# Token mixers of a hybrid decoder trunk: a head's last turns as a task of their own, beside the opening of the next head

## The chip, the cores and the metric

The kernel runs on 1 core of a Trainium2 chip, as one program in one launch. The metric is device time in microseconds (us), the median of the runs. A profiled execution of the kernel before is at hand: it names for each engine (PE is TensorE, DVE is VectorE, ACT is ScalarE, POOL is GpSimd, SP issues most transfers) each instruction with its start, its length and what it waited for.

## The reference, cut to what matters

One layer, a sequence of 1024 tokens, width 2048, all in float32:

```python
h = x @ w_in[i]                      # 15 column blocks of 512
y_a = short_conv_mixer(a_b, a_c, a_x, conv_w[i])
y_b = hgrn2_mixer(b_q, b_f, b_i, lower_bounds[i], hgrn_norm_g[i])      # 4 heads, state 128x128
y_c = diff_attn_mixer(c_q, c_k, c_v, lam, lam_init, diff_norm_g[i])    # 4 heads of 128
y_d = spatial_gate_mixer(gelu(d_u), gelu(d_v), ...)
y = concat([y_a * silu(g_a), y_b * silu(g_b), y_c * silu(g_c), y_d * silu(g_d)]) @ w_out[i]
x = layer_norm(ALPHA * x + y)
x = x + (p[i] @ w_pe[i]) * sigmoid(x @ w_pg[i])
```

`diff_attn_mixer` takes `softmax(q1 k1) - lam * softmax(q2 k2)`, causal, times v; `hgrn2_mixer` is a gated recurrence computed in blocks. The output of each head of B and of C goes through an RMS norm over its 128 channels before it is gated.

## The kernel before, in words

The three large products (`w_in`, `w_out`, `w_pg`) run as Strassen products: seven products of half matrices in place of eight, each of them as three matmuls of a high and a low part (`split`, lines 139 and 140: ACT casts a tile to `hi`, DVE subtracts to get `lo`). The `w_in` product runs in two stages. Stage one (up to some 690 us) takes four of the seven products for each of 30 groups of two column tiles (`PAIRS`) and puts the sums aside. Stage two (`second(g)`, 690 to 1430 us) takes the other three, of 24 matmuls each, and finishes the columns of group g. The order of `PAIRS` is C head 0, C head 1, the blocks of D, C heads 2 and 3, then for each j the B head j and the A channels j.

The token mixers are computed beside stage two. Each is a Python generator in `queue`; `products(..., every=2)` calls `step()` after every sixth matmul, and a step runs the generator at the head of the queue up to its next `yield`. So a stretch of mixer work stands behind every six matmuls of the product, 12 steps in a group, and a bare `yield` gives six matmuls of time to what went before. `unit_c(j)` and `unit_b(j)` enter the queue when their last columns are done (`kept(g, more)`). Only the head of the queue runs; a unit that enters waits until those ahead have ended.

A C head (`unit_c`, `mix_c`) loads its k, v and q tiles from DRAM (`back`, POOL's queue), waits 4 yields, splits k and q (casts L725, L726, L728, L737 on ACT, subtractions L727, L738 on DVE), transposes v (`turned`, L532), and then goes through eight blocks of queries: scores (L759, L760), softmax (L772, L782), transposes of the probabilities (`turn`, L791, into the tile `W`), times v (`values`, L798). At the end the gate is loaded (`gate_back`, L563), `rms(o, ss)` norms (L542 on DVE, a power on POOL L544, L545 on DVE), seven bare yields follow, and `finish` transposes the output (L552, tile `yt`), multiplies it with the gate (L554) and stores it to `y_dram` (L555). A B head (`unit_b`, `mix_b`) has the same frame around seven levels (L648 to L658, `gram` L617, L632), the transposes of its k (L532), and the state (`upd`, `hgo`, L681 to L703).

The tiles of one head are in the pool `work` under tags with one buffer each (`o`, `l1`, `q1`, `k1`, `v1`, `a1`, `x1`, `vt`, `W`) and `E` with two. A tile is written anew only when all who use what it held have ended, transfers included. In a C head `o` holds first the raw k and then the output; the gate is loaded to `l1` (C) or `v1` (B); a B head writes its product to `o` and keeps its output in an `E`.

The order on each engine is set when the program is built: the layer that builds it takes, for each engine, the instruction that stands first in the program among those that it holds to be ready by its own estimate; `early()` moves loads and splits of the large products ahead. Each engine then runs its list strictly in that order, whatever has really arrived.

After stage two the last unit (B head 3) runs on beside the first `w_out` product (L437, `tk`), and `drain()` puts out what is left of it before the tiles of A and B are loaded.

Of the kernel before, what the change touches and what calls it, by code (L numbers as in the profile page):

```python
# [38 lines left out]
def trunk_kernel(  # L39
# [79 lines left out]

    queue = []

    def step():
        while queue:
            if next(queue[0], queue) is not queue:
                return
            queue.pop(0)

    def drain():  # L130
        while queue:
            step()

    early = lambda: tc.high_priority(offset=4000)
# [330 lines left out]
    with tc.tile_pool(name="work", bufs=1) as work:  # L465
# [57 lines left out]
        def back(b, j, t):  # L523
            nc.gpsimd.dma_start(t, h_dram[b, j])
            return t
# [21 lines left out]
        def finish(o, norm, gt, y, kb):  # L547
            gt, y = ch(gt), ch(y)
            for b in range(2):
                ps = mx.tile([P, 4, P], F32, tag="mx", name="yt")  # L550
                for c in range(4):
                    T.transpose(ps[:, c, :], o[:, 4 * b + c, :], ident)  # L552
                c4 = slice(4 * b, 4 * b + 4)
                V.scalar_tensor_tensor(y[:, c4, :], ps, norm, gt[:, c4, :], op0=ALU.mult, op1=ALU.mult)  # L554
            nc.sync.dma_start(y_dram[kb].rearrange("p (c t) -> p c t", t=P), y)  # L555
# [5 lines left out]
        def gate_back(tag, k):  # L561
            gt = wt(tag)
            nc.gpsimd.dma_start(gt, g_dram[k])  # L563
            return gt
# [23 lines left out]
        def unit_b(j):  # L588
            k, f, qt, lw = wt("k1"), back(B_F, j, wt("l1")), back(B_Q, j, wt("q1")), wtE()
            iv = back(B_I, j, wtE())  # L590
            for _ in range(4):
                yield
            S.activation(k, f, AF.Sigmoid, scale=-1.0)
            S.activation(f, f, AF.Sigmoid)
            S.activation(k, k, AF.Copy, scale=one_lb[:, j : j + 1])
            V.tensor_scalar(f, f, one_lb[:, j : j + 1], lb[:, j : j + 1], op0=ALU.mult, op1=ALU.add)
            V.tensor_scalar_max(lw, f, SPLIT)
            V.tensor_scalar(f, f, F_FLOOR, SPLIT, op0=ALU.max, op1=ALU.min)
            S.activation(lw, lw, AF.Ln)
            S.activation(f, f, AF.Ln, scale=1.0 / SPLIT)  # L600
            V.tensor_tensor(f, f, lw, op=ALU.add)
            yield
            vtok = turned(wt("vt"), iv)
            yield
            yield from mix_b(j, k, f, qt, vtok)

        def mix_b(j, kt, lt, qt, vtok):
            at = ch(wt("a1"))
            G.memset(at, 0.0)

            def gram(li, m, ls, rs):
                if m >= 32:
# [58 lines left out]
            yield  # L671
            ktok = ch(wtV())
            transpose_to(ktok, ch(kt))
            o = ch(wtE())
            yield
            state = None
            ss = small.tile([P, 8], F32, tag="ss", name="ss")
            for b in range(2):
# [25 lines left out]
                S.copy(o[:, 4 * b : 4 * b + 4, :], pso)  # L704
                for c in range(4):
                    square(ss, 4 * b + c, pso[:, c, :])
            gt = gate_back("v1", 4 + j)
            rms(o, ss)
            for _ in range(7):
                yield  # L710
            finish(o, hg_g(j), gt, wt("o"), 4 + j)

        def unit_c(j):
            kraw, vraw, qraw = back(C_K, j, wt("o")), back(C_V, j, wtE()), back(C_Q, j, wtE())
            for _ in range(4):
                yield
            kh = [wt(t, dt=F32R) for t in ("l1", "q1")]
            kl = [wt(t, dt=F32R) for t in ("k1", "v1")]  # L720
            for mp in range(2):
                own = slice(64 * mp, 64 * mp + 64)
                oth = slice(64 - 64 * mp, 128 - 64 * mp)
                src, hi = kraw[own, :], kh[mp][own, :]
                S.copy(hi, src)  # L725
                S.copy(kh[mp][oth, :], src)  # L726
                V.tensor_tensor(kl[mp][own, :], src, hi.bitcast(F32), op=ALU.subtract)  # L727
                S.copy(kl[mp][oth, :], kl[mp][own, :].bitcast(F32))  # L728
            yield
            vtok = turned(wt("vt"), vraw)  # L730
            yield
            qs = [wt(t, dt=F32R) for t in ("a1", "x1")]
            for mp in range(2):
                own = slice(64 * mp, 64 * mp + 64)
                oth = slice(64 - 64 * mp, 128 - 64 * mp)
                src, hi = qraw[own, :], qs[mp][own, :]
                S.copy(hi, src)  # L737
                V.tensor_tensor(qs[mp][oth, :], src, hi.bitcast(F32), op=ALU.subtract)  # L738
            yield
            yield  # L740
            yield
            yield from mix_c(j, kh, kl, qs, vtok)

        def mix_c(j, kh, kl, qs, vtok):
# [59 lines left out]
            for i in range(NCH):  # L804
                a_t, rc = scores(i)
                yield
                if last is not None:
                    values(*last)
                if i >= 2:
                    yield  # L810
                last = (i, turn(i, a_t), rc)
                if i >= 4:
                    yield
            yield
            values(*last)
            gt = gate_back("l1", j)
            rms(o, ss)
            for _ in range(7):
                yield
            finish(o, da_g[:, j : j + 1], gt, gt, 8 + j)  # L820

        vd = []

# [400 lines left out]
```

## Time and profile before

| | us |
|---|---|
| median of 3 runs (2148.4 to 2153.97) | 2150.9 |
| the profiled execution's own time | 2151.72 |
| its span, first to last instruction | 2149.9 |
| PE busy of it | 2049.5 (95%) |
| DVE, ACT busy | 1393.3, 872.6 |
| stage two with the mixers, 690 to 1485 us: PE busy | 738.7 of 795 |

A busy PE is one with a matmul in it. Where PE is idle, the trace names what it waited for: an instruction of another engine or a transfer. An engine that runs its list in order and waits at its head also holds back all that stands behind it.

### The profile page before, as it was taken

To read this page: it belongs to the slowest core of one execution; us is meant where nothing else is said; L and a number is where in the kernel's file an instruction comes from. 1 tells how busy PE (TensorE), PEld (TensorE's weight loads), DVE (VectorE), ACT (ScalarE), POOL (GpSimd) and SP (SyncE) were. 2 spreads that over 40 slices of the span, in tenths; PEclk is the share of its full clock that TensorE was granted. 3 is DMA by queue.
4 is the path that set the end of the run, shared out by engine and by line. 5 is a ranking of instruction groups with operands and counts; after the bars stand their busy time and mean duration, and the time that the engine had idled before them with its cause. 6 is when DMAs were issued, how large, how long until landed. Compare 5 with 4: busy or idle time off the path is not lost. (4 is left out here: it accounts for less than half of the span.)

```text
span 2149.9 us, 25562 instructions
## 1 busy us (share of the span) xinstructions
PE 2049.5 (95%) x9708; PEld 1686.0 (78%) x9708; DVE 1393.3 (65%) x1763; ACT 872.6 (41%) x1287; POOL 150.2 (7%) x224
## 2 busy tenths in 40 slices
PE   7999999999999999988999989988999999999989
PEld 5788888878787777777878878867878788888867
DVE  7644545455465365756666778886767999455785
ACT  4322222222224256753555555553322245533432
POOL 0000101101010000010000000000121100000000
PEclk9999999999999999999999999999999999999999
DMA  6666767767778656467455364585677643433564
GB/s 236 238 201 219 265 229 266 268 236 258 250 261 306 224 168 194 128 216 250 156 166 195 124 208 145 195 307 195 238 280 254 233 167 102 153 98 99 189 204 136
DMA packets 169755, 443.81 MB, mean 206 GB/s; under 512 B 14432, under 2 KB 14576, under 8 KB 168352
## 3 DMA queue, kind: packets, MB, share of 16 engines
q1 hardware_dynamic: 120928, 293.05, 41.5%
q0 software_dynamic: 28064, 101.93, 13.3%
q10 hardware_dynamic: 20640, 47.19, 5.7%
q8 instruction: 76, 1.25, 0.3%
q14 instruction: 47, 0.39, 0.1%
HBM read 311.05 MB, written 131.07 MB: 206 GB/s over the span
## 5 line engine op out<-in xcount | busy, mean ns | idle before, releaser
L139 ACT CAST wh<-b 128x1024 fp32r<-128x1024 f32 x180 | 189.1, 1051 | 528.4 <-PE a L188 344.5
L437 PE MATMUL tk<-th,ah 128*128 128x512 f32 x832 | 327.0, 396 | 5.8 <-DVE z L967 3.0
L437 PE MATMUL tk<-th,al 128*128 128x512 f32 x832 | 325.8, 392 | 6.1 <-DVE al L140 5.9
L437 PE MATMUL tk<-tl,ah 128*128 128x512 f32 x832 | 322.7, 393 | 3.8 <-DVE tl L140 3.8
L140 DVE TENSOR_TENSOR wl<-b,wh 128x1024 fp32r<-128x1024 f32 x180 | 219.8, 1222 | 158.2 <-ACT wh L139 152.4
L437 PEld LDWEIGHTS tk<-th,ah 128*128 128x128 f32 x832 | 156.9, 189 | 40.5 <-issue 3.4
L437 PEld LDWEIGHTS tk<-th,al 128*128 128x128 f32 x832 | 157.0, 189 | 40.2 <-DVE al L140 9.0
L437 PEld LDWEIGHTS tk<-tl,ah 128*128 128x128 f32 x832 | 156.9, 189 | 38.0 <-DVE tl L140 5.0
L139 ACT CAST th<-t 128x1024 fp32r<-128x1024 f32 x64 | 67.4, 1054 | 206.5 <-PE tk L437 185.4
L262 DVE TENSOR_TENSOR b<-b,b 128x1024 f32<-128x1024 f32 x30 | 36.8, 1225 | 160.9 <-DMA b<-in_w_in_dram 160.9
L140 DVE TENSOR_TENSOR tl<-t,th 128x1024 fp32r<-128x1024 f32 x64 | 78.0, 1222 | 57.9 <-ACT th L139 57.8
L139 ACT CAST th<-b 128x1024 fp32r<-128x1024 f32 x48 | 50.6, 1053 | 140.6 <-PE tk L437 106.6
L188 PE MATMUL b<-N1h,wh 128*128 128x512 f32 x240 | 97.0, 404 | 7.5 <-ACT wh L139 7.5
L188 PE MATMUL a<-A22h,wl 128*128 128x512 f32 x240 | 96.2, 401 | 8.3 <-DVE wl L140 8.2
L188 PE MATMUL a<-S2h,wh 128*128 128x512 f32 x240 | 95.2, 397 | 6.3 <-ACT wh L139 5.3
L188 PE MATMUL a<-S2h,wl 128*128 128x512 f32 x240 | 95.1, 396 | 3.5 <-DVE wl L140 3.5
L188 PE MATMUL a<-S2l,wh 128*128 128x512 f32 x240 | 95.0, 396 | 3.4 <-DVE S2l L140 3.4
L188 PE MATMUL c<-A12h,wh 128*128 128x512 f32 x240 | 96.5, 402 | 1.7 <-ACT wh L139 1.7
L188 PE MATMUL b<-N1h,wl 128*128 128x512 f32 x240 | 96.5, 402 | 1.0 <-DVE wl L140 1.0
L188 PE MATMUL c<-A12h,wl 128*128 128x512 f32 x240 | 96.7, 403 | 0.0
L188 PE MATMUL c<-A12l,wh 128*128 128x512 f32 x240 | 96.4, 402 | 0.0
L188 PE MATMUL b<-N1l,wh 128*128 128x512 f32 x240 | 96.3, 401 | 0.0
(337 smaller groups left out, 4611.9 us busy)
## 6 DMA issues: line engine op xcount, KB each, us to landing
b<-in_w_in_dram SPq DMA_DIRECT2D x182, 512.0 KB, 4.6
stash<-ev ACTq DMA_DIRECT2D x60, 512.0 KB, 4.2
e<-stash SPq DMA_DIRECT2D x60, 512.0 KB, 4.7
s<-in_w_out_dram POOLq DMA_DIRECT2D x32, 512.0 KB, 7.4
ot<-s POOLq DMA_DIRECT2D x32, 512.0 KB, 5.5
h<-e SPq DMA_DIRECT2D x32, 512.0 KB, 4.6
t<-ot SPq DMA_DIRECT2D x32, 512.0 KB, 4.5
t<-b ACTq DMA_DIRECT2D x30, 512.0 KB, 3.9
```

Of the source, the lines that this page charges most:

```text
L139: S.copy(hi, raw)
L140: V.tensor_tensor(lo, raw, hi.bitcast(F32), op=ALU.subtract)
L188: T.matmul(ps, lhsT=w_[:, c], rhs=x_[k // 4][:, k % 4, :], start=(start and k == 0 and i3 == 0), stop=(k == 7 and i3 == 2), skip_group_che ...
L262: V.tensor_tensor(b22, b22, b12, op=ALU.add)
L437: T.matmul(ps[nn][m], lhsT=l[:, kk % 2, t], rhs=w[:, wi, :], start=(not cont and kk == 0 and i3 == 0), stop=(kk == 7 and i3 == 2), skip_gr ...
```

## The change

`finish` leaves the generators. When a head has normed its output, it puts `finish` with a counter of 9 into a new list `later`; `step()` counts it down and runs it 9 steps on, beside what the queue then does. One turn before its end a head calls `open_next()`, which runs the next generator in the queue, if there is one, up to its first `yield`: that is its loads. The opening yields become 5.

So that two heads can be open at once, the tiles move: a C head loads its raw k into `a1` (not `o`), the gate of B and C goes to `W`, where `finish` also writes the product; a B head keeps its output in `o` (not an `E`); `turns` starts from 0 in each B head, so that its first level takes `x1` and then `W`. In `unit_c` q is loaded ahead of v, and the transposes of v come after the split of q and three bare yields, with four behind them. No instruction of computation is added or taken away.

```diff
--- before.py
+++ after.py
@@ -119,16 +119,27 @@
 
 
 
-    queue = []
+    queue, later = [], []
 
     def step():
+
+        for todo in list(later):
+            todo[0] -= 1
+            if todo[0] == 0:
+                later.remove(todo)
+                todo[1]()
         while queue:
             if next(queue[0], queue) is not queue:
                 return
             queue.pop(0)
 
+    def open_next():
+
+        if len(queue) > 1:
+            next(queue[1])
+
     def drain():
-        while queue:
+        while queue or later:
             step()
 
     early = lambda: tc.high_priority(offset=4000)
@@ -588,7 +599,7 @@
         def unit_b(j):
             k, f, qt, lw = wt("k1"), back(B_F, j, wt("l1")), back(B_Q, j, wt("q1")), wtE()
             iv = back(B_I, j, wtE())
-            for _ in range(4):
+            for _ in range(5):
                 yield
             S.activation(k, f, AF.Sigmoid, scale=-1.0)
             S.activation(f, f, AF.Sigmoid)
@@ -607,6 +618,7 @@
         def mix_b(j, kt, lt, qt, vtok):
             at = ch(wt("a1"))
             G.memset(at, 0.0)
+            turns[0] = 0
 
             def gram(li, m, ls, rs):
                 if m >= 32:
@@ -671,7 +683,7 @@
             yield
             ktok = ch(wtV())
             transpose_to(ktok, ch(kt))
-            o = ch(wtE())
+            o = ch(wt("o"))
             yield
             state = None
             ss = small.tile([P, 8], F32, tag="ss", name="ss")
@@ -704,17 +716,16 @@
                 S.copy(o[:, 4 * b : 4 * b + 4, :], pso)
                 for c in range(4):
                     square(ss, 4 * b + c, pso[:, c, :])
-            gt = gate_back("v1", 4 + j)
+            open_next()
+            gt = gate_back("W", 4 + j)
             rms(o, ss)
-            for _ in range(7):
-                yield
-            finish(o, hg_g(j), gt, wt("o"), 4 + j)
+            later.append([9, lambda: finish(o, hg_g(j), gt, gt, 4 + j)])
 
 
 
         def unit_c(j):
-            kraw, vraw, qraw = back(C_K, j, wt("o")), back(C_V, j, wtE()), back(C_Q, j, wtE())
-            for _ in range(4):
+            kraw, qraw, vraw = back(C_K, j, wt("a1")), back(C_Q, j, wtE()), back(C_V, j, wtE())
+            for _ in range(5):
                 yield
             kh = [wt(t, dt=F32R) for t in ("l1", "q1")]
             kl = [wt(t, dt=F32R) for t in ("k1", "v1")]
@@ -727,8 +738,6 @@
                 V.tensor_tensor(kl[mp][own, :], src, hi.bitcast(F32), op=ALU.subtract)
                 S.copy(kl[mp][oth, :], kl[mp][own, :].bitcast(F32))
             yield
-            vtok = turned(wt("vt"), vraw)
-            yield
             qs = [wt(t, dt=F32R) for t in ("a1", "x1")]
             for mp in range(2):
                 own = slice(64 * mp, 64 * mp + 64)
@@ -736,9 +745,11 @@
                 src, hi = qraw[own, :], qs[mp][own, :]
                 S.copy(hi, src)
                 V.tensor_tensor(qs[mp][oth, :], src, hi.bitcast(F32), op=ALU.subtract)
-            yield
-            yield
-            yield
+            for _ in range(3):
+                yield
+            vtok = turned(wt("vt"), vraw)
+            for _ in range(4):
+                yield
             yield from mix_c(j, kh, kl, qs, vtok)
 
         def mix_c(j, kh, kl, qs, vtok):
@@ -811,13 +822,12 @@
                 last = (i, turn(i, a_t), rc)
                 if i >= 4:
                     yield
+            open_next()
             yield
             values(*last)
-            gt = gate_back("l1", j)
+            gt = gate_back("W", j)
             rms(o, ss)
-            for _ in range(7):
-                yield
-            finish(o, da_g[:, j : j + 1], gt, gt, 8 + j)
+            later.append([9, lambda: finish(o, da_g[:, j : j + 1], gt, gt, 8 + j)])
 
         vd = []
```

What stands on POOL where C head 0 ends and C head 1 opens, before (with buffer numbers; `h8_1`, `h6_1`, `h7_1` are v, q and k of head 1, `g_dram0` the gate of head 0):

```order
L563 DMA l1_5758<-g_dram0_97 128x1024
L524 DMA E_5828<-h8_1_4821 128x1024
L524 DMA E_5830<-h6_1_4825 128x1024
L544 ISA
L544 TENSOR_TENSOR rstd_5761<-ss_5211,nhalf_115 128x8
L524 DMA o_5826<-h7_1_4817 128x1024
```

The same place on POOL with the change:

```order
L535 DMA a1_5764<-h7_1_4817 128x1024
L535 DMA E_5766<-h6_1_4825 128x1024
L535 DMA E_5768<-h8_1_4821 128x1024
L574 DMA W_5795<-g_dram0_97 128x1024
L555 ISA
L555 TENSOR_TENSOR rstd_5798<-ss_5245,nhalf_115 128x8
```

The load of k stood behind the norm's power and waited for `o`; now it stands first, q ahead of v, and the gate goes to `W`.

PE at the same place, before: the last products ahead of the transposes of head 0's output and of head 1's v (`pv` of the last block is 40 product matmuls ahead):

```order
L188 MATMUL c_6068<-A12h_4676,wh 128x512
L188 MATMUL c_6068<-A12l_4678,wh 128x512
L188 MATMUL c_6068<-A12h_4676,wl 128x512
L552 MATMUL yt<-ident,o 128x128 x8
L532 MATMUL tr<-ident,E 128x128 x8
L188 MATMUL c_6068<-A12h_4676,wh 128x512
```

PE with the change, from that `pv` on:

```order
L809 MATMUL pv<-vt,W 128x128 x8
L199 MATMUL b_5673<-N4l_4759,wh 128x512
L199 MATMUL b_5673<-N4h_4757,wl 128x512
L199 MATMUL b_5673<-N4h_4757,wh 128x512
L199 MATMUL b_5673<-N4l_4759,wh 128x512
L199 MATMUL b_5673<-N4h_4757,wl 128x512
L199 MATMUL c_6068<-A12h_4675,wh 128x512
L199 MATMUL c_6068<-A12l_4677,wh 128x512
L199 MATMUL c_6068<-A12h_4675,wl 128x512
L543 MATMUL tr<-ident,E 128x128 x8
```

The transposes of v (`tr`) now come 8 product matmuls after the last `pv`; head 0's `yt` follows 33 more behind them, and head 1's first scores right behind it.

DVE where B head 0 makes its first level, before (`W` is the second tile of that level):

```order
L601 TENSOR_TENSOR l_8680<-l_8680,E 128x1024
L511 TENSOR_TENSOR e_20_8901<-b_8904,e_20_8901 128x512
L571 TENSOR_TENSOR e_20_8900<-e_20_8900,e_20_8901 128x1024
L140 TENSOR_TENSOR wl<-t_22_9294,wh 128x1024
L648 TENSOR_TENSOR x_8762<-q_8682,E 128x512
L649 TENSOR_TENSOR x_8762<-q_8682,E 128x512
L650 TENSOR_TENSOR W<-k_8679,E 128x1024
L658 TENSOR_TENSOR l_8680<-l_8680 128x512
```

DVE there with the change, from the norm of C head 3 on:

```order
L553 TENSOR_SCALAR ss<-ss 128x8
L556 TENSOR_TENSOR o<-o,rstd 128x1024
L565 SCALAR_TENSOR_TENSOR W<-yt,da_g,W 128x512
L612 TENSOR_TENSOR l_8558<-l_8558,E 128x1024
L565 SCALAR_TENSOR_TENSOR W<-yt,da_g,W 128x512
L151 TENSOR_TENSOR wl<-t_20_8972,wh 128x1024
L660 TENSOR_TENSOR x_8671<-q_8560,E 128x512
L661 TENSOR_TENSOR x_8671<-q_8560,E 128x512
L670 TENSOR_TENSOR l_8558<-l_8558 128x512
L522 TENSOR_TENSOR e_18_8591<-b_8594,e_18_8591 128x512
L662 TENSOR_TENSOR W<-k_8557,E 128x1024
L664 TENSOR_TENSOR E<-l_8558 128x256x2
```

The first level came long after C head 3's product with the gate; now it comes directly behind it and writes `W`, which that product has just filled for the store to `y_dram`.

PE at the end of B head 3, beside the `w_out` product, before:

```order
L437 MATMUL tk_10832<-tl,ah 128x512
L532 MATMUL tr<-ident,k_10531 128x128 x8
L681 MATMUL upd<-vt,W 128x128 x4
L686 MATMUL hgo<-vt,a_10609 128x128 x4
L703 MATMUL hgo<-state,q_10534 128x128 x3
L681 MATMUL upd<-vt,W 128x128 x3
L686 MATMUL hgo<-vt,a_10609 128x128 x4
L703 MATMUL hgo<-state,q_10534 128x128 x4
L552 MATMUL yt<-ident,E 128x128 x8
L437 MATMUL tk_11157<-th,ah 128x512
```

PE there with the change, right behind the last `hgo`:

```order
L448 MATMUL tk_10826<-th,al 128x512
L448 MATMUL tk_10826<-tl,ah 128x512
L448 MATMUL tk_10827<-th,ah 128x512
L448 MATMUL tk_10827<-th,al 128x512
L448 MATMUL tk_10827<-tl,ah 128x512
L448 MATMUL tk_10828<-th,ah 128x512
L448 MATMUL tk_10828<-th,al 128x512
L448 MATMUL tk_10828<-tl,ah 128x512
L448 MATMUL tk_10829<-th,ah 128x512
L448 MATMUL tk_10829<-th,al 128x512
L448 MATMUL tk_10829<-tl,ah 128x512
L563 MATMUL yt<-ident,o 128x128 x8
```

Eleven product matmuls of the `w_out` product now stand between the last state product and the transposes of the normed output.

## Rows read from the trace of the kernel before

**Rows 1.** Windows: PE, PEld, DVE, ACT, POOL busy us (instructions), granted clock, DMA share.

```profile
300.00:350.00 50.00, 50.00 (x222) 41.32 (x221) 27.57 (x24) 15.19 (x20) 6.28 (x10) 1.00 0.74 262
690.00:1485.00 795.00, 738.69 (x3901) 613.07 (x3901) 533.06 (x881) 429.13 (x751) 47.02 (x61) 0.97 0.57 191
1410.00:1455.00 45.00, 36.84 (x226) 30.51 (x227) 43.15 (x58) 22.03 (x28) 0.00 (x0) 1.00 0.85 300
1470.00:1485.00 15.00, 10.43 (x39) 8.76 (x40) 4.37 (x6) 2.58 (x9) 4.58 (x5) 0.77 0.56 176
```

**Rows 2.** Waits of PE, 690 to 1500 us: total, times, longest.

```profile
PE yt L552 <- DVE o L545: 7.8, 4, 3.2
PE yt L552 <- DVE E L545: 7.7, 3, 5.5
PE b L188 <- ACT wh L139: 7.5, 2, 4.7
PE gram L632 <- DVE x L650: 5.5, 2, 3.7
PE sc L759 <- DVE a L738: 4.7, 1, 4.7
PE sc L759 <- ACT l L726: 4.5, 2, 2.6
PE tk L437 <- DVE al L140: 3.6, 2, 2.9
PE gram L617 <- DVE W L657: 3.5, 1, 3.5
...
PE yt L552 <- ACT wh L139: 1.0, 1, 1.0
```

**Rows 3.** Timeline of PE, end of C head 0: start, length, engine, line.

```profile
832.12 1.06 PE L791 MATMUL att<-ident,E 128*128 128x128 f32 x8
833.47 2.05 PE L798 MATMUL pv<-vt,W 128*128 128x128 f32 x16
847.80 1.22 PE L552 MATMUL yt<-ident,o 128*128 128x128 f32 x8 [3.20 <-DVE o L545]
```

**Rows 4.** Timeline of POOL: loads of the next C head.

```profile
832.49 0.53 POOL L524 DMA_DIRECT2D E<-h  x1 [13.18 <-DMA e<-stash]
...
849.32 0.59 POOL L524 DMA_DIRECT2D o<-h  x1 [10.41 <-PE yt L552]
...
1081.50 0.53 POOL L524 DMA_DIRECT2D E<-h  x1 [7.95 <-DMA b<-in_w_in_dram]
```

**Rows 5.** Timeline of ACT: casts that waited for those loads.

```profile
841.20 1.05 ACT L737 CAST a<-E 64x1024 fp32r<-64x1024 f32 x1 [4.92 <-DMA E<-h]
...
1005.98 1.05 ACT L725 CAST l<-o 64x1024 fp32r<-64x1024 f32 x1 [7.20 <-DMA o<-h]
...
1087.73 1.04 ACT L737 CAST a<-E 64x1024 fp32r<-64x1024 f32 x1 [1.36 <-DMA E<-h]
```

**Rows 6.** Timeline of PE, end of B head 3.

```profile
1468.06 1.06 PE L703 MATMUL hgo<-state,q 128*128 128x128 f32 x8
1474.57 1.94 PE L552 MATMUL yt<-ident,E 128*128 128x128 f32 x8 [5.46 <-DVE E L545]
```

**Rows 7.** DMA issues of a kind: KB each, median us to landing.

```profile
E<-h POOLq DMA_DIRECT2D x16, 512.0 KB, 5.3
```

**Rows 8.** Line L555, the stores of a head's product.

```profile
DMA to landing us min/median/max: 2.7/5.7/7.1
```

**Rows 9.** Timeline of DVE, first level of B head 0.

```profile
1208.28 1.22 DVE L140 TENSOR_TENSOR wl<-t,wh 128x1024 fp32r<-128x1024 f32 x1
1209.87 0.69 DVE L648 TENSOR_TENSOR x<-q,E 128x512 f32<-128x512 f32 x1 [0.37 <-ACT E L646]
```

**Rows 10.** Timeline of SP's queue: a weight load and the transfer behind it.

```profile
743.07 0.39 SPq L173 DMA_DIRECT2D b<-in_w_in_dram  x1
755.86 0.32 SPq L490 DMA_DIRECT2D t<-t  x1
```

## The prediction, made before the change was run

> **What bounds the kernel now.** I read the windows first. In a stretch of products alone PE is busy for all of 50 us, with 222 matmuls, so 0.225 us for one. In the mixer stretch it is busy 738.7 of 795 us [rows 1]: TensorE is the bound, and 56 us of its idle time lie there. DVE (533 us) and ACT (429 us) have room in the mean, though not at the end, where DVE is busy 43.2 of 45 us. PE's work does not change, so the change can only move those 56 us, and the time in which the granted clock is down: it is 0.77 in the last window of rows 1, so part of it at 1.2 GHz, after a wait.
>
> Next, what the 56 us wait for [rows 2]. The transposes of a head's normed output (`yt`) have 7.8 + 7.7 + 1.0 = 16.5 us. The first scores of a C head (`sc`) have 4.7 + 4.5 = 9.2, and the split that ACT does late beside them (`b <- wh`) 7.5, of which I put some 1.7 to the opening of C head 2. The levels of the B heads and the product beside the last one have 5.5 + 3.5 + 3.6 = 12.6. The first two are what the change speaks of.
>
> Last, how one of them comes about. At the end of C head 0 PE has its last `pv` done at 833.47 + 2.05 = 835.5 and reaches `yt` at 844.6, and waits 3.20 us [rows 3]. ACT had stood 4.92 us for the next head's q, whose load POOL issued at 832.5 and which the cast took at 841.2, 8.7 us later [rows 4, 5]; DVE's subtraction for q stands ahead of the norm and waits with it. The load of k is issued only at 849.3, when `yt` has freed `o` [rows 4], so the first scores wait too. An engine that waits for a load holds back everything behind it, and these loads are slow.
>
> **The change part by part.** A step is six matmuls, 1.35 us. Counted in the code, a C head holds the queue for 35 steps before (4+1+1+3, 18 in the blocks, 1, 7) and 31 now until the next one is opened; a B head 39 and 32. But a unit can't start before its columns are done: B head 3 is opened at step 341 in both, and its levels begin at step 348 instead of 347. The queue's total is no shorter. What counts is where the order puts each instruction. All sums are against the profiled execution's own 2151.72 us (the span of 2149.9 and 1.8 around it), which is 0.8 above the median of 2150.9.
>
> *Waits of `yt`: -10.5.* For the four C heads `yt` now comes 41, 10, 10 and 10 product matmuls after the last `pv` and behind the eight transposes of the next tile (1.0 us), against 40, 18, 14 and 11; it is not later in matmuls, but the wait below comes ahead of it and covers the norm. I set the four at nothing (7.8 before). For the B heads the distance from the last state product is 16, 16, 54 and 11 matmuls and for the first of them 1.0 us of transposes as well, against 21, 19, 23 and 0. At the end of B head 3 the norm takes from 1469.1 to 1474.6 = 5.5 us with nothing to cover it [rows 6]; 11 x 0.225 = 2.5 now cover it, 3.0 stay. I leave 1.0, 2.0, 0 and 3.0. So 16.5 go to 6.0. Bounds: -14 (only the last stays) and -5 (half of them stay).
>
> *Transposes of the next v: +7.5.* These are new waits. The tile `E` is free when the last probabilities are transposed, or one instruction before, when DVE has read it; then the load is issued, and PE needs it after 0.45 + 2.05 + 1.8 = 4.3 us (C head 0: two products, `pv`, eight products), 4.3 (C head 2), 4.7 and 4.1 (before B head 0 and D, where the tile is free 1.1 earlier): 17.4 us of cover in all. Four loads at the median of 5.3 [rows 7] and 0.1 each to issue make 21.6, so 4.2 of waits; at the 8.7 of 832.5 to 841.2 they make 34.8, so 17.4. I take the 6.2 us from 1081.50 to 1087.73 [rows 4, 5], the opening of C head 3 and the less crowded of the two cases: 24.8 - 17.4 = 7.4, taken as 7.5. The Trainium skill (DMA: Bandwidth & Descriptors, Anatomy of one DMA) gives a transfer issued by GpSimd about 2.0 us and its bytes at 436 GB/s, an estimate of 3.2 us for 512 KB; by it these waits and 7.5 us of the sum would be gone. The trace disagrees: the median is 5.3 us. Its main page (Trainium Kernel Development and Optimization, Key Constraints) says that all queues share the same 16 DMA engines, so that an earlier issue brings no bandwidth; that fits the 8.7 us, and it would take the sum to the upper end.
>
> *First scores of a C head: -6.8.* k no longer waits for `o`. The opening of C head 0 stays, since its columns set it. That of C heads 1 and 3 stands 41 and 10 matmuls and two sets of transposes behind the last `pv`, with k loaded before: 4.5 go. C head 2 loses the 7.20 us in which ACT stood for k [rows 5], but its q is stored only some six steps before it is split, and a cast for it may stand ahead of a split again. Of 4.7 + 1.7 + 4.5 = 10.9 I leave 4.1. Bounds: 0 and -10.9.
>
> *Casts of the next k: +2.* On ACT they now stand ahead of the copies of the last probabilities (C heads 1 and 3). k's load can be issued when `a1` is free, after the last scores; at 6.2 us the cast holds ACT for some 1 us each time. Bounds: 0, and +5 at 8.7 us for both.
>
> *The tile `W`: +2.4.* The gate, the product and its store hold `W`, and the next head's first write of `W` waits for the store: two copies on ACT (C heads 1 and 3), two multiplications on DVE (B heads 0 and 1). Behind B head 0's stand the next split and the copies of the levels. The store takes 0.3 to issue and 5.7 [rows 8]; the order has one split of 1.2 and four instructions of 0.7 between [rows 9], 4 us: 2 us. The copies have 25 to 28 matmuls and the scores, 7 to 8 us, against 1.4 for the products and 6.0: 0.2 each. B head 1 has 70 matmuls. Bounds: 0 (the store at 2.7) and +8 (at 7.1, and held in SP's queue).
>
> *Levels of the B heads: -3.2.* Between the last `pv` of C head 3 and the last `yt` lie 838 matmuls before and 878 now, and the levels of B head 0 start 141 earlier, those of B head 3 14 earlier (3.2 us). Where DVE is full, that takes 3.2 us off the 12.6. Bounds: -8 and +2.
>
> The sum is -10.5 + 7.5 - 6.8 + 2 + 2.4 - 3.2 = -8.6: 2143.1, and 0.8 less for the median: 2142.3. I forecast 2142 us.
>
> **The rivals.** *The loads take the place of the norm: no change.* If the loads take 8.7 us, as at the first boundary, the new waits are 17.4 instead of 7.5: -8.6 + 9.9 = +1.3, 2152. For it: these openings load three tiles and a gate in a row. Against it: 6.2 at the other one. The same outcome, at 2148, if `open_next()` finds an empty queue where it matters: it does so at B heads 1 to 2 and 2 to 3.
>
> *The tile `W`: slower.* SP's queue can stand long ahead of a store: after the weight load at 743.07 the next transfer is issued at 755.86, 12.8 us later [rows 10]. A store of a product behind such a load holds `W`, then DVE or ACT, then the splits behind them. With 6.0 for the store less some 5 of work between, the engine stands 13.8; a product of 24 matmuls already split covers 5.4, so PE loses 8.4 at a place. At two of the four places that is +16.8, less the 2.4 I have counted: 2142 + 14 = 2156. It decides from some 5 us at two places. Against it: the stores before follow the product closely, and the loads in front of them are few.
>
> *More goes than I count:* loads at the median, no first scores that wait, nothing for k and `W`: -10.5 + 4.2 - 10.9 - 3.2 = -20.4, 2130.5.
>
> **How the numbers follow.** My case, -6.5 to -20, has 0.50. More than that 0.05. No change 0.25 (loads 0.18, empty queue 0.07). Slower 0.20 (`W` 0.14; 0.06 for the casts of k or q that hold ACT before more splits than I see). About 0.3%, 6.5 us, is what a measurement of this kernel can tell from no change. So faster 0.55, same 0.25, slower 0.20. The range that holds 8 in 10 reaches from 2129 to 2156; the likeliest case's own is 2131 to 2144.
>
> **What would show it.** In the profile after: PE's wait at `yt` for C heads under 1 us, 3 us at the last; a new wait of the transposes of v (`tr <- E`) of 1 to 4 us at the end of C heads 0 to 3; first scores of C heads 1 and 3 without a wait, and no cast of k that stands 7 us; the first level of B head 0 some 30 us earlier against the products, DVE standing about 2 us for a store there; PE idle from 690 to 1485 near 48 us instead of 56. I am wrong if DVE or ACT stand more than 5 us for `y_dram` at more than one place, if the waits of `tr` come to over 15 us, or if the last 60 us of stage two have as much idle time as before.

## The result and the profile after

The changed kernel takes 2126.48 us (median; 2126.28 to 2130.34), the kernel before 2149.65 beside it: ratio 0.9891, 95% interval 0.9862 to 0.9921. So it is faster, by 23 us where 8.6 were forecast, and below the range of 2129 to 2156.

Windows of the changed kernel: first two that answer to [rows 1], then the mixer stretch, from the first wait of stage two to the `yt` of B head 3.

```profile
690.00:1485.00 795.00, 753.79 (x3989) 626.28 (x3989) 547.33 (x898) 437.99 (x760) 46.23 (x61) 0.98 0.59 199
1410.00:1455.00 45.00, 40.43 (x253) 33.53 (x252) 35.52 (x48) 24.80 (x42) 3.70 (x4) 0.96 0.64 223
698.01:1449.04 751.03, 716.26 (x3840) 596.25 (x3841) 520.75 (x872) 425.03 (x746) 43.27 (x57) 0.98 0.57 194
```

The same stretch of the kernel before, cut at the same two instructions:

```profile
697.79:1474.57 776.78, 723.28 (x3840) 600.54 (x3841) 524.59 (x873) 421.77 (x742) 45.51 (x59) 0.97 0.56 188
```

Both do 3840 matmuls. The stretch is 25.7 us shorter: PE's idle time falls from 53.5 to 34.8 (-18.7), and its busy time by 7.0, at a granted clock of 0.98 for 0.97. The rest of the program is 3.9 us longer (2128.3 - 1449.04 against 2149.9 - 1474.57). DVE, full at the end of stage two before, is busy 35.5 of the 45 us there.

PE's waits of the changed kernel, 690 to 1500 us; they answer to [rows 2] (total, times, longest):

```profile
PE b L199 <- ACT wh L150: 11.4, 4, 3.5
PE yt L563 <- DVE o L556: 8.3, 4, 2.9
PE tr L844 <- DMA E<-h: 3.9, 2, 3.2
PE tr L543 <- DMA E<-h: 3.2, 2, 1.9
...
PE tk L448 <- ACT ah L150: 2.6, 1, 2.6
PE tk L448 <- DVE al L151: 2.2, 2, 1.2
...
PE gram L644 <- DVE W L669: 1.6, 1, 1.6
PE pv L809 <- ACT W L803: 1.3, 2, 0.8
PE gram L644 <- DVE W L662: 0.8, 1, 0.8
...
PE gram L629 <- DVE W L669: 0.3, 1, 0.3
```

No row of first scores is left, the levels (`gram`) have 2.7 us, and the new row is `tr` behind a load of `E`, 7.1 us in all. The product beside the last head (`tk`) waits no less than before, 4.8 us for 4.5; but 3.6 of them now come at 1475.98 and 1477.77, behind the last `yt`, and so lie in the 3.9 us above.

The timeline of PE and POOL where C head 0 ends; it answers to [rows 3, 4]:

```profile
824.55 0.53 POOL L535 DMA_DIRECT2D a<-h  x1 [81.39 <-DVE mxs L775]
...
835.01 0.53 POOL L535 DMA_DIRECT2D E<-h  x1 [9.92 <-DMA e<-stash]
835.99 0.53 POOL L535 DMA_DIRECT2D E<-h  x1 [0.45 <-PE att L802]
...
836.00 2.04 PE L809 MATMUL pv<-vt,W 128*128 128x128 f32 x16
...
841.18 1.09 PE L543 MATMUL tr<-ident,E 128*128 128x128 f32 x8 [1.30 <-DMA E<-h]
...
849.62 0.60 PE L563 MATMUL yt<-ident,o 128*128 128x128 f32 x4
```

k is asked for at 824.55 instead of 849.32, and `yt` no longer waits; v, asked for at 835.99, is waited for instead. The end of B head 3, which answers to [rows 6], waits 2.91 us instead of 5.46:

```profile
1449.04 1.94 PE L563 MATMUL yt<-ident,o 128*128 128x128 f32 x8 [2.91 <-DVE o L556]
```

One wait is new in a place that the prediction does not speak of, in B head 3. Timeline of POOL, DVE, ACT and PE:

```profile
1367.74 0.53 POOL L535 DMA_DIRECT2D q<-h  x1 [7.59 <-DMA h<-e]
...
1375.01 0.69 DVE L660 TENSOR_TENSOR x<-q,E 128x512 f32<-128x512 f32 x1 [7.25 <-DMA q<-h]
...
1377.53 0.70 ACT L666 ACTIVATE E<-l 128x512 f32<-128x512 f32 x1 [11.19 <-DVE W L662]
1378.11 1.06 ACT L150 CAST wh<-t 128x1024 fp32r<-128x1024 f32 x1
...
1379.22 0.50 PE L199 MATMUL b<-N1h,wh 128*128 128x512 f32 x1 [3.52 <-ACT wh L150]
```

The columns of q have only just been stored (`h<-e`) when POOL loads them: the mixers have caught up with the product that feeds them. DVE stands for q, ACT for DVE, and the next weight cast stands behind that on ACT: 3.5 + 0.6 us of PE's time.

### The profile page after: what moved, and what is told of

Same layout as the page of the kernel before. It is cut to its first block, busy times and chain, and to the rows that moved or that the text cites. A ratio compares the mean times of both kernels' runs of the same rounds, so it can differ in the third digit from the quotient of the medians.

```text
span 2128.3 us, 25560 instructions
## 1 busy us (share of the span) xinstructions
PE 2045.9 (96%) x9708; PEld 1684.5 (79%) x9708; DVE 1391.3 (65%) x1763; ACT 876.1 (41%) x1291; POOL 149.7 (7%) x224
## 5 line engine op out<-in xcount | busy, mean ns | idle before, releaser
L199 PE MATMUL b<-N1h,wh 128*128 128x512 f32 x240 | 98.9, 412 | 11.4 <-ACT wh L150 11.4
L199 PE MATMUL a<-A11h,wh 128*128 128x512 f32 x240 | 94.5, 394 | 1.9 <-ACT A11h L150 1.9
L199 PE MATMUL a<-A11l,wh 128*128 128x512 f32 x240 | 94.7, 395 | 1.1 <-DVE A11l L151 1.1
L199 PE MATMUL b<-N4h,wh 128*128 128x512 f32 x240 | 95.1, 396 | 0.0
```

Source lines behind the costliest of these rows:

```text
L199: T.matmul(ps, lhsT=w_[:, c], rhs=x_[k // 4][:, k % 4, :], start=(start and k == 0 and i3 == 0), stop=(k == 7 and i3 == 2), skip_group_che ...
```

## The experiments

All ratios are to the kernel before, run on the same chip. The "gap" is the time from the first `yt` of C head 3 to the first `gram` of B head 0; it is 32.3 us before (1180.13 to 1212.44).

**The parts of the change.** First the tile layout alone:

```diff
-            kraw, vraw, qraw = back(C_K, j, wt("o")), ...
+            kraw, vraw, qraw = back(C_K, j, wt("a1")), ...
-            gt = gate_back("l1", j)
+            gt = gate_back("W", j)
-            o = ch(wtE())
+            o = ch(wt("o"))
-            gt = gate_back("v1", 4 + j)
+            gt = gate_back("W", 4 + j)
-            finish(o, hg_g(j), gt, wt("o"), 4 + j)
+            finish(o, hg_g(j), gt, gt, 4 + j)
+            turns[0] = 0
```

> The kernel before with the tile layout of the change alone: raw k in a1, the gates in W, a B head's output in o, turns from 0; finish stays in the generator behind seven yields, nothing is opened early, unit_c keeps its order and the four yields. Theory tiles (the waits of the B heads' levels fall because an output no longer holds one of the two E and a gate no longer holds l1): most of the gain is here, 2126 to 2137 us, and PE's waits at gram and tk fall from 15 us to about 5. Theory overlap (they fall because the next head is opened while the last one ends): 2143 to 2152 us, gram and tk still 10 us or more, first scores of C heads 1 and 3 somewhat earlier since k no longer waits for o.

Measured: 2121.23, 0.9865 [0.9842, 0.9887]: by the medians 5 us more than the whole change gave, though the two intervals overlap. In its mixer stretch PE is idle 27.9 us:

```profile
693.82:1436.50 742.68, 714.83 (x3841) 595.48 (x3841) 521.94 (x872) 421.37 (x743) 42.77 (x57) 0.99 0.57 196
```

The opposite, the changed kernel without the moves in time (layout, new order of a C head's opening and five opening yields stay):

```diff
-            open_next()
-            later.append([9, lambda: finish(...)])
+            for _ in range(7):
+                yield
+            finish(...)
```

> The change without its two moves in time: finish behind seven yields inside the generator and no open_next, in B and C heads; the tile layout, unit_c's new order of loads and transposes and the five opening yields stay. A head holds the queue for 39 to 40 steps again. Theory overlap: 2143 to 2155 us (the same as before or a little slower, since a C head is four steps longer). Theory tiles: 2126 to 2138 us.

Measured: 2133.27, 0.9915 [0.9888, 0.9941]. The new opening costs the layout 12 us: it holds the queue four steps longer in each C head and one in each B head, and by the order the levels of the last B head begin at product matmul 5109 instead of 4980, where `drain()` comes at 5136 (counted in the traces). Three rows of its waits of PE name them:

```profile
PE gram L644 <- DVE W L662: 4.1, 2, 3.3
PE gram L644 <- DVE x L669: 4.0, 1, 4.0
...
PE gram L629 <- DVE W L669: 2.7, 1, 2.7
```

The changed kernel with the moves in C heads alone, so that edit in `mix_b` only:

```diff
-            open_next()
             gt = gate_back("W", 4 + j)
...
-            later.append([9, lambda: finish(o, hg_g(j), gt, gt, 4 + j)])
+            for _ in range(7):
+                yield
+            finish(o, hg_g(j), gt, gt, 4 + j)
```

> The change with open_next and the late finish in C heads alone; a B head finishes inside its generator behind seven yields and opens nothing; all tiles as in the change. Theory overlap: C head 3 opens B head 0 early, so that the B heads have more room although they don't overlap each other: about two thirds of the gain, 2131 to 2139 us; yt waits of B heads as before (about 8 us), no first-score waits. Theory tiles: within 4 us of the change, 2124 to 2131 us.

Measured: 2126.25, 0.9883 [0.9865, 0.9901]. And in B heads alone, the edit in `mix_c` only:

```diff
-            open_next()
             yield
             values(*last)
...
-            later.append([9, lambda: finish(o, da_g[:, j : j + 1], gt, gt, 8 + j)])
+            for _ in range(7):
+                yield
+            finish(o, da_g[:, j : j + 1], gt, gt, 8 + j)
```

> The change with open_next and the late finish in B heads alone; a C head finishes inside its generator behind seven yields and opens nothing; all tiles as in the change. Theory overlap: only B head 1 is opened early (the queue is empty at the others), so little of the gain: 2138 to 2148 us. Theory tiles: 2124 to 2133 us.

Measured: 2119.28, 0.9852 [0.9834, 0.9871]. So the layout is what pays, and the moves in time mend what the new opening costs it. For the moves in B heads alone that is clear of the intervals (0.9852 against 0.9915), for all of them together (0.9891) it is not.

**Which tile.** One line each in the kernel before. The gate of a C head:

```diff
-            gt = gate_back("l1", j)
+            gt = gate_back("W", j)
```

> The kernel before with one tile moved: the gate of a C head is turned into tile W instead of l1. In the order of the instructions the first level of B head 0 moves from product matmul 4441 to 4318, since its load of f into l1 no longer waits for the end of C head 3, and the four B heads spread over some 120 products more. Theory 'gate in l1' (the levels of the B heads were waited for because they were squeezed behind C head 3): most of the 34 us that the layout alone gained in the mixers comes back here, 2125 to 2135, with the waits for levels and gates of B heads down from some 16 us to under 6. Theory 'output in E' (the gain came from B's output no longer holding one of the two E tiles): within 5 us of the kernel before, 2145 to 2155.

Measured: 2128.14, 0.9894 [0.9869, 0.9918], as much as the whole change, by one word. A B head's output:

```diff
-            o = ch(wtE())
+            o = ch(wt("o"))
-            finish(o, hg_g(j), gt, wt("o"), 4 + j)
+            finish(o, hg_g(j), gt, gt, 4 + j)
```

> The kernel before with one tile moved: a B head's output lies in tile o instead of one of the two tiles E, and its gate is finished in place. The order moves little: the second to fourth B head open 2 to 27 products earlier. Theory 'output in E': 10 us or more faster, 2130 to 2140, with the waits at the B heads' levels mostly gone. Theory 'gate in l1': 2145 to 2152, levels waited for as before.

Measured: 2144.25, 0.9985 [0.9964, 1.0007]: nothing that can be told from no change. A C head's raw k:

```diff
-            kraw, vraw, qraw = back(C_K, j, wt("o")), ...
+            kraw, vraw, qraw = back(C_K, j, wt("a1")), ...
```

> The kernel before with one tile moved: raw k of a C head goes into tile a1 instead of o, so that its load does not wait for the head before to be done with its output. Theory 'first scores' (a C head's first scores wait because k comes late): the waits of the first scores, 10.9 us in the kernel before, fall by 5 to 9, and the time to 2141 to 2146. Theory 'gate in l1': not more than 4 us, 2146 to 2152.

Measured: 2140.57, 0.9945 [0.9927, 0.9962], some 12 us, about what the theory of the first scores had. But its reason does not hold: the first scores do fall to 1.4 us, the transposes of v wait 12.0 us for loads of `E` instead, and up to the first `yt` of C head 3 PE is idle 30.0 us, before 28.7. The gain lies behind that: 13.6 us idle from the first level of B head 0 on, before 24.4. 23 and 12 us for the two tiles are more than the 29 of the whole layout, by less than the intervals leave open; so whether they overlap is not shown.

How the gate's tile does it is seen on the timelines around the end of C head 3. SP, POOL and PE of the kernel before:

```profile
1182.26 0.32 SPq L555 DMA_DIRECT2D y_dram<-l  x1
...
1187.18 0.59 POOL L524 DMA_DIRECT2D l<-h  x1 [8.37 <-DVE wl L140]
...
1212.44 2.02 PE L632 MATMUL gram<-x,W 128*128 128x128 f32 x16 [0.40 <-DVE W L650]
```

The tag `l1` holds the gate and then the product of C head 3, until its store has landed. B head 0's f belongs in `l1` too, and its load goes out 4.9 us after that store was issued; the row names a split on DVE for it, `wl`, that does not touch `l1`. In the run with k moved alone, where `l1` is used as before, the same row names the store:

```profile
1185.35 0.59 POOL L524 DMA_DIRECT2D l<-h  x1 [9.35 <-DMA y_dram<-l]
```

With the gate in `W` (POOL, PE):

```profile
1158.88 0.53 POOL L524 DMA_DIRECT2D l<-h  x1 [65.08 <-PE sc L760]
...
1182.59 2.02 PE L632 MATMUL gram<-x,W 128*128 128x128 f32 x16
```

The load waits for nothing but the last scores, f is there before head 3 has ended, the first level stands at product matmul 4318 of the order instead of 4441, and the gap shrinks from 32.3 us to 7.2 (1175.35 to 1182.59). What that is worth, windows of the kernel before, in the gap and from it to the last `yt`:

```profile
1181.22:1212.44 31.22, 30.82 (x140) 25.33 (x139) 17.55 (x21) 20.79 (x21) 0.59 (x1) 1.00 0.50 169
1212.44:1474.57 262.13, 237.69 (x1463) 201.30 (x1464) 217.44 (x306) 141.56 (x221) 17.26 (x21) 0.98 0.55 189
```

The same two windows with the gate in `W`:

```profile
1176.44:1182.59 6.15, 6.14 (x32) 4.88 (x30) 5.86 (x8) 3.60 (x5) 0.00 (x0) 1.00 0.50 162
1182.59:1454.65 272.06, 262.83 (x1586) 221.76 (x1587) 226.54 (x317) 153.82 (x231) 17.36 (x21) 1.00 0.59 198
```

In the gap PE is busy all the time (30.8 of 31.2 us): it runs products, and no wait is recorded but the last 0.4. But 140 matmuls are spent there beside a mixer that stands. The four B heads, whose own matmuls are the same, then have 123 fewer beside them (1463 against 1586), and PE is idle 24.4 us there instead of 9.2. The gap is paid for in the 262 us behind it.

The fourteen kernels here bear that out in part. From the first level to the last `yt`, the six with 1463 to 1495 matmuls have 13.6 to 25.5 us of idle time on PE, the eight with 1563 to 1609 have 9.1 to 15.0. So the matmuls that are left go with the idle time, but they do not fix it. The kernel with the moves in B heads alone has the first level at 4411, near the 4441 of before, with a gap of 7.5 us (1178.28 to 1185.78); 1494 matmuls and 15.2 us idle follow, and it is fast. The changed kernel without its moves in time has 4411 and a gap of 7.5 too, and 25.5 us. And the one with k alone moved keeps a gap of 28.8 us and has 13.6. What else decides is open.

That the gate alone comes to the figure of the whole change is chance, since it saves in other places. Windows up to the first `yt` of C head 3: the kernel before, the gate in `W`, the change; then the change from its first level on:

```profile
697.79:1180.13 482.34, 453.68 (x2230) 372.82 (x2230) 289.20 (x547) 259.41 (x501) 27.65 (x37) 0.96 0.57 190
699.79:1175.35 475.56, 446.75 (x2215) 368.94 (x2215) 288.53 (x548) 268.57 (x509) 27.12 (x38) 0.97 0.56 191
698.01:1156.70 458.69, 439.19 (x2196) 363.06 (x2197) 286.21 (x546) 266.32 (x509) 26.67 (x37) 0.98 0.57 194
1165.87:1449.04 283.17, 268.72 (x1604) 226.44 (x1605) 227.09 (x317) 153.33 (x231) 16.61 (x20) 0.99 0.58 197
```

Up to there PE is idle 28.7, 28.8 and 19.5 us, from the first level on 24.4, 9.2 and 14.5. What the gate's tile saves of idle time lies in the B heads alone; of what the change saves, half lies in the C heads, of which the prediction spoke most. The changed kernel with the gate left in `l1` was not run.

**The moves in time.** The changed kernel with the old opening of a C head:

```diff
-            kraw, qraw, vraw = back(C_K, j, wt("a1")), back(C_Q, j, wtE()), back(C_V, j, wtE())
-            for _ in range(5):
+            kraw, vraw, qraw = back(C_K, j, wt("a1")), back(C_V, j, wtE()), back(C_Q, j, wtE())
+            for _ in range(4):
...
+            vtok = turned(wt("vt"), vraw)
+            yield
...
-            vtok = turned(wt("vt"), vraw)
-            for _ in range(4):
-                yield
```

> The changed kernel with the opening of a C head in its old order (v loaded before q, v turned before q is split, four turns before it) and all the rest of the change. Theory 'the new order of the opening costs' (the layout with the new opening and no moves in time was 12 us slower than the layout alone): 2112 to 2120. Theory 'the moves in time cost' (a late end and an early opening take what the layout gave): 2124 to 2130, as the changed kernel.

Measured: 2134.63, 0.9923 [0.9895, 0.995], slower than both theories have it. With both moves the old opening gains 16.5 us on the kernel before by the medians, the new one 23.2; the intervals overlap by most of their length, so that it is worse here is not shown. Without the moves it is better by 12. One wait on ACT's timeline is long:

```profile
981.69 1.04 ACT L736 CAST l<-a 64x1024 fp32r<-64x1024 f32 x1 [11.48 <-DMA a<-h]
982.64 1.04 ACT L150 CAST wh<-b 128x1024 fp32r<-128x1024 f32 x1
```

ACT stands 11.5 us for k, and the weight cast stands behind it; PE's waits for `wh` come to 15.4 us in this kernel. But this k is that of C head 2, which follows the blocks of D and which no head opens early; the kernel without `open_next()`, next, has 8.1 us at the same place. So the row is no sign of what early loads cost. Then each move without the other, in the changed kernel. Without `open_next()`, which was to take the early loads away:

```diff
     def open_next():
-        if len(queue) > 1:
-            next(queue[1])
+        pass
```

> The changed kernel without the early loads: open_next does nothing, the late end of a head stays. Theory 'early openings put loads' casts in front of weight casts on ScalarE' (a load that has not landed holds ScalarE, and the cast of the next weights behind it): the waits of products for wh fall from 11.4 us to 5 or less, and the time to 2117 to 2122. Rival 'the openings hide first scores and turns of v': those waits come back at the head's starts, 2130 to 2136.

Measured: 2117.36, 0.9846 [0.9822, 0.9869], the lowest ratio of all, 9 us below the changed kernel by the medians. But the edit does not take the early loads away. POOL and PE of this run at the end of C head 0:

```profile
821.95 0.53 POOL L534 DMA_DIRECT2D a<-h  x1 [81.81 <-DVE mxs L774]
832.40 0.53 POOL L534 DMA_DIRECT2D E<-h  x1 [9.92 <-DMA e<-stash]
833.39 0.53 POOL L534 DMA_DIRECT2D E<-h  x1 [0.45 <-PE att L801]
833.40 2.04 PE L808 MATMUL pv<-vt,W 128*128 128x128 f32 x16
```

k, q and v of the next head go out 11.45, 1.00 and 0.01 us ahead of the last `pv`, as in the changed kernel (824.55, 835.01 and 835.99 to 836.00). With the late end a generator is over in its last turn and the same step opens the next head, so the call only brings the turns of the next opening forward by one; in a B head it stands in that last turn itself. In the layout alone the three loads go out ahead of the end of that `pv` too, and so in every run with this layout. What late loads would do to it no run shows.

The waits of PE, the rows of weights and of v:

```profile
PE b L198 <- ACT wh L149: 6.5, 3, 2.8
PE tr L843 <- DMA E<-h: 6.1, 2, 3.5
PE b L198 <- DVE wl L150: 5.2, 3, 3.0
```

`wh` falls from 11.4 to 6.5, near the 5 that was expected, but not for the reason expected: 3.5 of the 4.9 us are the wait behind B head 3's q (1379.22 above), and that place has this row here:

```profile
1370.60 0.50 PE L198 MATMUL b<-N1h,wl 128*128 128x512 f32 x1 [2.98 <-DVE wl L150]
```

B head 3 is not opened early: POOL has its loads in the same order with the call and without it, behind the gate of B head 2. The transposes of v wait no more than with the call (6.1 and 0.5 in another row, against 7.1), and the stretch takes 743.34 us instead of 751.03. The call kept, but the end in its old place:

```diff
-            later.append([9, lambda: finish(...)])
+            for _ in range(7):
+                yield
+            finish(...)
```

> The changed kernel with each head's last turns in their old place, seven turns of the queue behind the norm and ahead of the next head; the early loads stay. By the order the B heads then come later and are squeezed at the end (the last one's first level at product matmul 5044 instead of 4986). Theory 'late end frees the mixers' chain': slower than the changed kernel, 2130 to 2136, with the waits at levels of the last head back. Rival 'the late end gives nothing': 2124 to 2129.

Measured: 2126.14, 0.9879 [0.9854, 0.9904], the rival's number: beside the call the late end gives nothing that can be told. Last, on the layout alone with the old opening, the late end in B heads only, with a counter of 6:

```diff
             rms(o, ss)
-            for _ in range(7):
-                yield
-            finish(o, hg_g(j), gt, gt, 4 + j)
+            later.append([6, lambda: finish(o, hg_g(j), gt, gt, 4 + j)])
```

> The tile layout of the change alone (old order of the opening of C heads), and of the moves only the late end of B heads, 6 turns behind the norm; no early loads. If the waits of B heads' last turns for the norm (half of the 12.3 us that the layout alone still has) go and nothing else moves: 2114 to 2118, faster than both. If the last product waits are set by what the last head needs, and not by these: 2119 to 2124, as the layout alone.

Measured: 2125.9, 0.9886 [0.9864, 0.9907], above both of the figures expected. And that with the call of `open_next()` in B heads and a counter of 8:

```diff
+            open_next()
             gt = gate_back("W", 4 + j)
             rms(o, ss)
...
-            later.append([6, lambda: finish(o, hg_g(j), gt, gt, 4 + j)])
+            later.append([8, lambda: finish(o, hg_g(j), gt, gt, 4 + j)])
```

> As the layout alone with the late end of B heads (8 turns) and also their early loads. Theory 'B heads gain by both': 2112 to 2117. Rival 'early loads hold ScalarE and VectorE behind a load that has not landed': slower than with the late end alone, 2120 to 2128, with waits for wh of over 8 us in the windows of the B heads.

Measured: 2125.88, 0.9887 [0.9862, 0.9912]. It waits 12.2 us for `wh`, but 8.0 of them at 700 and 757 us, before the first B head; the rival asked for more than 8 in the B heads' windows, where there are 4.2. It is no slower than the late end alone. Neither beats the layout alone.

| layout, and | no move | `open_next` | late end | both |
|---|---|---|---|---|
| new opening | 0.9915 | 0.9879 | 0.9846 | 0.9891 (the change) |
| old opening | 0.9865 | not run | not run | 0.9923 |

So the layout with the new opening and the late end beats both kernels by its median (2117.36), and its interval and the change's share only 0.9862 to 0.9869. That it also beats the layout alone is not shown: those intervals overlap by most of their length.

## Why the prediction was wrong

The direction was right, and the reason was not. Step by step, PE's waits before and after:

| step | predicted | measured |
|---|---|---|
| waits of `yt` | -10.5 | 16.5 to 8.3: -8.2 |
| transposes of the next v | +7.5 | 7.1 new, 2.1 behind a multiplication on DVE gone: +5.0 |
| first scores | -6.8 | 10.9 to 2.9: -8.0 |
| casts of the next k | +2 | `pv` behind ACT at B head 0's opening: +0.8 |
| tile `W` | +2.4 | `pv` of C head 1: +0.5 |
| levels of the B heads | -3.2 | 16.2 to 7.5: -8.7 |
| granted clock | 0 | -7.0 of PE's busy time |
| not in the sum | | +4.1 (q of B head 3), -1.7 (opening of C head 0), +0.3 after the mixers beside `tk` |

The right column adds to -22.9; the spans differ by 21.6.

**The step that failed is the levels of the B heads**, with "Where DVE is full, that takes 3.2 us off the 12.6. Bounds: -8 and +2." With the smaller rows (`gram` 1.2, `upd` 1.5, `tk` 0.9) these are 16.2 us, and 7.5 are left: -8.7, past the bound. The levels (`gram`) fall from 10.2 to 2.7 and `upd` to nothing; `tk`, which I had among the 12.6, keeps its waits, 4.5 and 4.8. I had the fact that counts, the levels of B head 0 starting 141 matmuls earlier, and priced only the 14 by which the last head is earlier. As the run with the gate moved shows, a head start gives cover to all four heads (9.2 us idle for 24.4) and not only less lateness to the last, though the matmuls left are not the whole of it. And I did not ask why B head 0 was so late before: the gate in `l1`. I looked at the moved tiles for new waits alone (`W`, +2.4), and never at which load each tile that is left sets free. The move of that gate alone gives 0.9894, against 0.9891 for all. That two different edits reach the same figure does not make the change nothing else: the whole layout has 0.9865 by itself, the new opening costs that 12 us, and the moves in time seem to mend part of it.

**The clock** is the second step that failed: the sum has no term for it, although the first part said that the time at the lower level can move. The mixer stretch has 3840 matmuls in both, 723.28 us busy at 0.97 and 716.26 at 0.98, so less of it was granted the lower level, 1.2 GHz: 7.0 of the stretch's 25.7 us. Part of that is lost again: the first 193 matmuls from the last `yt` on have 0.90, the 192 before had 0.94, and over the whole execution PE's busy time falls by 3.7 us alone (2049.5 to 2045.9). What raised the clock in the stretch no run here shows.

**`yt`** was right in kind and place. I left 1.0, 2.0, 0 and 3.0 us for the B heads; they have 1.8, 1.8, 0 and 2.9, and C head 3 has 1.8 where I had nothing. But the late end does not earn this as time by itself: without it, and with the call of `open_next()` kept, the kernel is as fast (0.9879).

**The transposes of v** were right in size, at three of the four places (none waits before B head 0): 6.2 us was taken for a load, and the median of an `E<-h` load is 6.1 in the changed kernel, where [rows 7] have 5.3. The Trainium skill (DMA: Bandwidth & Descriptors, Anatomy of one DMA) puts such a transfer at an estimate of 3.2 us; by that these waits would not be there, and the trace disagrees here as before. Without `open_next()` they come to 6.6.

**First scores** were right; that k waits for `o` is borne out by the run with k alone in `a1`, which has 1.4 us of them left. The 1.7 us that I took for the opening of C head 2 are not in the 7.5 of `b <- wh`, which stand at 697.79 and 753.67; they are a row of `c` of the same size, at 1011.36.

**The tile `W`** cost 0.5 us, and the slower rival falls with it. After the store of C head 3's product at 1159.94 DVE writes `W` at 1164.51 without a wait; in C head 1 ACT does stand for the store, 3.17 us, and PE for 0.54 of them. The timelines of DVE there, and of ACT and PE in C head 1:

```profile
1163.91 0.69 DVE L522 TENSOR_TENSOR e<-b,e 128x512 f32<-128x512 f32 x1
1164.51 1.22 DVE L662 TENSOR_TENSOR W<-k,E 128x1024 f32<-128x1024 f32 x1
...
858.28 0.27 ACT L803 COPY W<-att 128x128 f32<-128x128 f32 x1 [3.17 <-DMA y_dram<-W]
858.60 0.49 PE L809 MATMUL pv<-vt,W 128*128 128x128 f32 x2 [0.54 <-ACT W L803]
```

The queue of SP did not hold that store long, which is what the rival needed. **The rival of the loads** did not come: a median of 6.1 us is far from its 8.7, and the waits of `tr` are 7.1 instead of its 17.4. What `open_next()` costs beside the late end (0.9891 against 0.9846, intervals that just overlap) is not the loads, which stand where they stood, and the order on ACT is not shown to be it: in the longest of those waits, for B head 3's q, no early load is in play. Without the late end the call seems to gain (0.9879 against 0.9915, intervals that overlap). Why stays open, and so does why the late end is worth some 15 us with the new opening and without the call (0.9846 against 0.9915), and nothing with it.

## What to carry to other kernels

When tiles move, list for each tag what it held, until which store, and which load wanted it next: the tile that is set free can be worth more than the move in time that it was made for. A gap in the work that is run beside a product can show no wait on TensorE where it stands and be paid for later, so count the product matmuls left beside each stage and not only the waits. Before crediting a reordering, run its layout by itself, and each of its moves with the others taken out; and look in the trace whether the move has moved what it was meant to move: here the loads went out at the same place with the call and without it.

## What the runs showed of the hardware

The granted clock does not go with the idle time of the same window alone. With the gate moved the B heads' window has 1.00 with 9.2 us idle of 272, and before it had 0.98 with 24.4 of 262, as one would think; but from 1410 to 1455 us the kernel before has 1.00 with 8.2 us idle [rows 1], and the changed one 0.96 with 4.6. And from 1470 to 1485 both have 0.77. I had not expected the clock to give 7.0 of the 25.7 us in the mixer stretch, and for another kernel I would look at it by stage.

The Trainium skill (Perfetto Trace Analysis, Identifying Performance Opportunities) says that gaps that repeat on the engine that should be saturated can mean a lack of buffers. The runs agree as to the cause, but no gap on TensorE marked the place: the buffer was short at 1180 us, and the gaps stood from 1212 to 1475 (24.4 us, and 9.2 with one tile moved).
